# Products that nobody reads in TensorE's planned idle time, and new prices in the planner

## The chip, the cores and the metric

The kernel runs on one core of a Trainium2 chip. The metric is the device time of one execution in microseconds (us), the median of several runs. TensorE (PE in the views) multiplies matrices into the banks of PSUM, VectorE (DVE), ScalarE (ACT) and GpSimd (POOL) do the element-wise work, and SyncE (SP) issues the DMA transfers. Each engine works through its own instructions in the order in which the program lists them; semaphores hold an instruction back until what it needs is there.

## What is computed

One inference step of a decoder of four layers over a prompt of 512 tokens and eight samples of 8 tokens, at a width of 1024, all in fp32:

```python
def trunk(x, st_gla, st_gdn, st_conv, st_re, st_im, wts):
    for i in range(DEPTH):                      # DEPTH = 4
        kind = i % N_MIXERS                     # 0 GLA, 1 gated DeltaNet, 2 S5
        if kind == 0:
            f, s = gla_mixer(x, ...)
        elif kind == 1:
            f, cv, s = gdn_mixer(x, ...)
        else:
            f, hr, hi = s5_mixer(x, ...)
        x = layer_norm(ALPHA_RES * x + f, wts['ln_g'][i], wts['ln_b'][i])
```

Layers 0 and 3 are gated linear attention (GLA) with four heads, layer 1 is the gated DeltaNet with eight heads, a short convolution and a triangular solve in each chunk, layer 2 is an S5 state space with a gated linear unit (GLU) behind it. Each layer ends in an output product, a residual and a layer norm, and the next layer needs the result. The final states are outputs too.

## The kernel before

Every weight matrix is streamed in units of 128x1024 words (512 KB). A unit is split into a high and a low part (a cast and a subtraction, on ScalarE or VectorE), and each unit's *dense products* run as three f32r products with 288, 256 or 512 columns; one record of the trace is one such product. Their tile is `ps<-fx`. All other products (`ps<-sb`) are plain fp32 products, which leave two records each, or transposes, which leave one.

Layer 1 works in four pairs of heads. For a pair, the convolved k and q go through transposes and scores (`gdn_scores`: 128x128 transposes, then 128x256 products, eight for a pair), VectorE solves the diagonal blocks (`gdn_solve`), and the heads finish on TensorE (`gdn_head`: 128x96, 96x96, 64x64 and 128x128 products, each waiting for an evacuation of the one before). The convolution takes three taps on VectorE for each k, q or v unit. Layer 2 works in four pairs of S5 blocks: 128x72 products, a scan on VectorE, 128x72 products again, a trip through DRAM (`Ud`, `Yd`), and then the GLU, whose first three units wait for each eighth of that result. The tables for S5 are prepared earlier by `s5_prep0`, which fills time in layers 0 and 1; its last and largest part is `s5_prep`, four times.

The order on every engine is the work of a planner at build time. Python generators (threads, each with a rank) record operations; `record` finds what each depends on, `cost` gives it a price in us, and `run` keeps a clock of its own and issues on each engine the ready operation with the lowest rank. The thread `dense` has rank 10 and so fills what the rest leaves; the split of weights has rank 5, the chunk work of a layer 3 and up. The program that reaches the chip holds this order and the semaphores, but none of the planner's times. `cp` sends a copy to VectorE or ScalarE, whichever has less planned work. In the views nearly all instructions carry one line, L379 (L407 after the change), the call in `issue`.

Of the kernel before, what the change touches and what calls it, by code (L numbers as in the profile page):

```python
# [19 lines left out]
P = 128  # L20
# [122 lines left out]
FIXED = KT * 4 * HW + KT * P + RING * 2048 + 512 + 2 * HW + 512  # L143
WORDS = 52992 - FIXED
BLOCK = object()
ENGINES = ('PE', 'DVE', 'ACT', 'POOL', 'SP')
ACT_SETS = {
    AF.Exp: ('exp_and_others', 'natural_log_exp_and_others'), AF.Ln: ('natural_log_exp_and_others',),
# [20 lines left out]
class Engine:  # L169


    def __init__(self, core, name, real):
        self.core, self.name, self.real = core, name, real
# [10 lines left out]
class Core:  # L184
# [5 lines left out]
    def __init__(self, ctx, tc):  # L190
        nc = self.real = tc.nc
        self.fixed = ctx.enter_context(tc.tile_pool(name="fx", bufs=1)).tile([P, FIXED], F32R, name="fx")
        self.sb = ctx.enter_context(tc.tile_pool(name="sb", bufs=1)).tile([P, WORDS], F32, name="sb")
        self.ps = ctx.enter_context(tc.tile_pool(name="ps", bufs=1, space=PSUM)).tile([P, 4096], F32, name="ps")
        self.dram_pool = ctx.enter_context(tc.tile_pool(name="dram", bufs=1, space=DRAM))
        self.sb_name, self.ps_name = self.sb.tensor.name, self.ps.tensor.name
        self.vector, self.scalar = Engine(self, 'DVE', nc.vector), Engine(self, 'ACT', nc.scalar)
        self.gpsimd, self.tensor = Engine(self, 'POOL', nc.gpsimd), Engine(self, 'PE', nc.tensor)
        self.sync = Engine(self, 'SP', nc.sync)
        self.clock = dict.fromkeys(ENGINES, 0.0)  # L200
        self.dma = 0.0
        self.pending = dict.fromkeys(ENGINES, 0.0)
        self.queue = {e: ([], []) for e in ENGINES}
        self.ops, self.now, self.table = [], 0.0, None
        self.dense_backlog = 0

        self.region = {}
        for name, n, g in ((self.sb_name, WORDS, 16), (self.fixed.tensor.name, FIXED, 16), (self.ps_name, 4096, 32)):
            self.track(name, n, g, 4)
        self.spans, self.scratch = {}, {}  # L210
        self.bank_op = {e: np.full((4, 8), -1, np.int32) for e in ENGINES}
        self.constants = set()
        self.holes, self.used = [[0, WORDS]], {}
        self.banks = [False] * 8
        self.frees = 0
        self.threads, self.seq, self.events = [], 0, set()
        self.cur = [None, 0, 0, None, '', lambda: 0]


    def track(self, name, n, g, rows):  # L220
        new = lambda: np.full((rows, n // g), -1, np.int32)
        self.region[name] = (n, g, new(), {e: new() for e in ENGINES})

# [28 lines left out]
    def record(self, eng, method, fn, args, kw):  # L252
# [19 lines left out]
        for v in outs:  # L272
            s = self.span(v)
            if s is not None:
                _, _, w, r = self.region[v.tensor.name]
                order.update(np.unique(w[s]).tolist())
                for e in ENGINES:
                    order.update(np.unique(r[e][s]).tolist())
# [47 lines left out]
    def cost(self, op, method, args, kw, outs, ins):  # L326

        eng = op.eng
        column = any(v.shape[-1] == 1 for v in ins) or len(outs) > 1
        if not outs:  # L330
            op.cost, op.table = 1.28, args[0]
            return
        out = outs[0]
        size = lambda v: prod(v.shape[1:])
        n = size(out) if eng == 'PE' else max(size(v) for v in outs + ins)
        if eng == 'PE':
            m = 0.107 * size(ins[0]) / P if method != 'transpose' else 0.0
            if method == 'transpose':
                op.cost = n * 0.85e-3
            elif kw['lhsT'].dtype == F32R:  # L340
                op.cost = max(n * 0.417e-3, m)
            else:
                op.cost = 2 * max(n * 0.833e-3, m)
        elif eng == 'DVE':
            in_ps = any(v.tensor.name == self.ps_name for v in outs + ins)
            op.cost = 0.07 + n / 960.0 * (0.5 if not in_ps and method in ('tensor_copy', 'tensor_scalar') else 1)
            if column:
                op.cost += 0.06
        elif eng == 'ACT':
            sb = all(v.tensor.name != self.ps_name for v in ins)  # L350
            op.cost = 0.05 + 0.835e-3 * n + (0.043 if sb else 0.0) + (0.093 if column else 0.0)
            op.table = ACT_SETS.get(args[2] if len(args) > 2 else None)
        elif eng == 'POOL':
            op.cost = 0.3 + 0.165 * n if kw.get('op') == ALU.pow else 0.12 + 2.2e-3 * n
            if method == 'memset':
                op.cost = 0.1 + 0.6e-3 * n
        else:
            op.cost, op.tail = 0.45, prod(out.shape) * 4 / 360e3

    def issue(self, op):  # L360
        e = op.eng
        t = max(self.now, op.ready)
        if op.table is not None:
            sets = op.table if isinstance(op.table, tuple) else (op.table,)
            if self.table not in sets:
                self.table = sets[0]
                if isinstance(op.table, tuple):
                    t += 1.28
        self.clock[e] = t + op.cost
        op.end = t + op.cost  # L370
        if e == 'SP':
            self.dma = max(self.dma, op.end + 0.7) + op.tail
            op.end = self.dma + 1.0
        op.issued = True
        self.pending[e] -= op.cost
        if e == 'PE' and op.rank >= 10:
            self.dense_backlog -= 1
        fn, args, kw = op.call
        fn(*args, **kw)  # L379
        op.call = None  # L380
        for s, lat in op.succ:
            s.ready = max(s.ready, t if lat is None else op.end + lat)
            s.pend -= 1
            if not s.pend:
                heappush(self.queue[s.eng][0], (s.ready, s.seq, s))
        op.succ = None

    def writers(self, *aps):
        ids = set()
        for v in aps:  # L390
            s = self.span(v)
            if s is not None:
                ids.update(np.unique(self.region[v.tensor.name][2][s]).tolist())
        ids.discard(-1)
        return [self.ops[i] for i in ids]
# [31 lines left out]
    def A(self, *shape, dt=F32, long=False):  # L427
        keep = self.cur[5]
        while True:
# [3 lines left out]
            if v is not None:  # L433
                return v
            yield BLOCK

    def bank(self, n=1, held=None):

        while True:
# [9 lines left out]
            if best is None:  # L449
                yield BLOCK  # L450
                continue
# [68 lines left out]
    def run(self):  # L520
        while True:
            wake = []
            moved = True
            while moved:
                moved, wake = False, []
                for th in list(self.threads):
                    c = self.can_go(th)
                    if c is not True:
                        if c is not False:
                            wake.append(c)  # L530
                        continue
                    self.cur = th
                    moved = True
                    try:
                        v = next(th[0])
                    except StopIteration:
                        self.threads.remove(th)
                        continue
                    if v is BLOCK:
                        v = self.frees  # L540
                    elif isinstance(v, bass.AP):
                        v = self.writers(v)
                    elif isinstance(v, list):
                        v = self.writers(*v)
                    th[3] = v
                for e in ENGINES:
                    waiting, ready = self.queue[e]
                    while waiting and waiting[0][0] <= self.now + 1e-9:
                        _, s, op = heappop(waiting)
                        heappush(ready, (op.rank, s, op))  # L550
                    if ready and self.clock[e] <= self.now + 1e-9:
                        self.issue(heappop(ready)[2])
                        moved = True
            for e in ENGINES:
                waiting, ready = self.queue[e]
                if ready:
                    wake.append(self.clock[e])
                elif waiting:
                    wake.append(max(self.clock[e], waiting[0][0]))
            wake = [t for t in wake if t > self.now]  # L560
            if not wake:
                if not self.threads:
                    return
                raise AssertionError("nothing can go on: " + str([t[4] for t in self.threads]) + str(self.banks))
            self.now = min(wake)
# [1757 lines left out]
```

## Time and profile before

| | |
|---|---|
| time, median of 3 runs (lowest to highest) | 1359.83 us (1357.68 to 1359.98) |
| the profiled execution's own time | 1360.72 us |
| its span, first to last instruction | 1358.9 us |
| TensorE busy | 1274.3 us (94%) |
| VectorE busy | 953.4 us (70%) |
| ScalarE busy | 601.9 us (44%) |
| granted clock of TensorE, mean | 0.960 |

The span is that of one execution under the profiler; the time around it is 1.8 us. The granted clock is 1 at 2.4 GHz and 0.5 at 1.2 GHz. Busy time of TensorE is modelled, so an engine that is busy for the whole of a stretch may still hold short waits; the number of its records in a stretch says how fast it went.

### The profile page before, as it was taken

The page shows a single profiled execution, that of the slowest core. Times are in us where ns is not written, and L with a number is a line of the kernel's source. Part 1 is how long each engine was busy: PE and PEld are TensorE (multiplying, and loading weights), DVE is VectorE, ACT ScalarE, POOL GpSimd, SP SyncE. Part 2 cuts the span into 40 slices and gives each one's busy share as a digit, 9 for nine tenths or more (in the row PEclk, how much of TensorE's full clock was granted, in tenths as well). Part 3 has the DMA queues.
Part 4 walks back from the last instruction along what each step waited for, and adds up shares of the span by engine and source line. Part 5 has one row for each costly group of instructions (what it writes and reads, how often), then busy time and mean ns, then how long its engine had stood idle before and what let it go on. Part 6 is the DMA issues. An engine that isn't in the chain of part 4 may idle for free.

```text
span 1358.9 us, 23510 instructions
## 1 busy us (share of the span) xinstructions
PE 1274.3 (94%) x8795; PEld 1193.2 (88%) x8795; DVE 953.4 (70%) x2087; ACT 601.9 (44%) x1341; POOL 163.0 (12%) x303
## 2 busy tenths in 40 slices
PE   8999998989996798899999889999999999999997
PEld 8999997869895698799988788999998899999985
DVE  5888888798999788778678519355334867665557
ACT  5554355224855665534542224346123245443430
POOL 5510000021211121112101000000000200000001
PEclk8999999989996899899999888899999999999999
DMA  6335546334456826274374598773325332332342
GB/s 233 106 106 167 183 149 209 128 103 141 126 147 192 235 65 189 54 177 131 118 246 128 186 238 211 202 197 86 109 78 178 104 122 98 129 129 98 124 147 70
DMA packets 129538, 198.35 MB, mean 146 GB/s; under 512 B 47176, under 2 KB 85961, under 8 KB 127377
## 3 DMA queue, kind: packets, MB, share of 16 engines
q1 hardware_dynamic: 129424, 196.86, 48.0%
q8 instruction: 69, 1.13, 0.4%
q14 instruction: 45, 0.36, 0.1%
HBM read 153.64 MB, written 47.37 MB: 148 GB/s over the span
## 4 chain that ended last, share of the span: by engine, by line
PE 76%; DVE 12%; DMA 5%; ACT 3%; issue 2%; SPq 2%; POOLq 0%; POOL 0%; DVEq 0%; ACTq 0%
PE ps L379 76%; DVE sb L379 9%; DVE fx L379 3%; ACT sb L379 2%; SPq L379 2%; DMA sb<-scr 1%; DMA sb<-Ud 1%; DMA sb<-in_s_z 1%; ACT fx L379 1%; DMA out_conv<-sb 0%; DMA sb<-in_gla_s 0%; DMA Ud<-sb 0%; DMA sb<-in_xT 0%; DMA Yd<-sb 0%; DMA sb<-in_gdn_s 0%
## 5 line engine op out<-in xcount | busy, mean ns | idle before, releaser
L379 PE MATMUL ps<-fx 128*128 128x288 f32 (+2 forms) x6736 | 1048.6, 313 | 21.1 <-DVE fx L379 7.9
L379 PEld LDWEIGHTS ps<-fx 128*128 128x128 f32 x6736 | 957.0, 192 | 70.8 <-DVE fx L379 10.4
L379 ACT CAST fx<-sb 128x1024 fp32r<-128x1024 f32 (+5 forms) x318 | 227.2, 743 | 315.9 <-PE ps L379 277.0
L379 DVE TENSOR_TENSOR fx<-sb,fx 128x1024 fp32r<-128x1024 f32 (+5 forms) x308 | 253.2, 846 | 158.1 <-ACT fx L379 143.3
L379 PE MATMUL ps<-sb 128*128 128x128 f32 (+10 forms) x2059 | 302.5, 299 | 54.1 <-DVE sb L379 20.2
L379 PEld LDWEIGHTS ps<-sb 128*128 128x128 f32 (+6 forms) x2059 | 252.7, 180 | 85.2 <-ACT sb L379 24.2
L379 DVE TENSOR_TENSOR sb<-sb 128x128 f32<-128x128 f32 (+32 forms) x667 | 262.0, 416 | 20.6 <-ACT sb L379 6.5
L379 ACT COPY sb<-ps 128x512 f32<-128x512 f32 (+10 forms) x247 | 94.4, 404 | 158.8 <-PE ps L379 96.8
L379 DVE SCALAR_TENSOR_TENSOR sb<-sb 128x600 f32<-128x600 f32 (+7 forms) x205 | 133.8, 661 | 13.2 <-ACT sb L379 6.9
L379 ACT ACTIVATE sb<-sb 128x128 f32<-128x128 f32 (+10 forms) x241 | 108.0, 501 | 65.8 <-DVE sb L379 57.5
L379 DVE SCALAR_TENSOR_TENSOR sb<-sb,ps 128x256 f32<-128x256 f32 (+3 forms) x216 | 92.9, 458 | 61.3 <-PE ps L379 44.7
L379 POOL TENSOR_TENSOR sb<-sb 128x1 f32<-128x1 f32 (+4 forms) x46 | 75.8, 1653 | 468.4 <-DVE sb L379 446.1
L379 ACT ACTIVATE sb<-ps 128x128 f32<-128x128 f32 (+2 forms) x176 | 67.0, 385 | 73.7 <-PE ps L379 42.9
L379 DVE SCALAR_TENSOR_TENSOR sb<-ps,sb 128x128 f32<-128x128 f32 (+3 forms) x112 | 55.7, 505 | 44.3 <-PE ps L379 40.7
L379 DVE COPY sb<-ps 128x256 f32<-128x256 f32 (+6 forms) x85 | 34.2, 407 | 66.0 <-PE ps L379 36.7
L379 POOL COPY sb<-sb 128x24 f32<-128x24 f32 (+4 forms) x92 | 35.9, 413 | 280.0 <-DVE sb L379 161.5
L379 POOL MEMSET sb<- 128x8 f32 (+9 forms) x96 | 28.5, 315 | 203.7 <-DVE sb L379 143.7
L379 ACT ACTIVATE sb<-ps,sb 128x128 f32<-128x128 f32 (+2 forms) x98 | 40.7, 435 | 22.6 <-PE ps L379 21.8
L379 ACT CAST fx<-ps 128x512 fp32r<-128x512 f32 (+2 forms) x32 | 17.6, 550 | 72.5 <-PE ps L379 69.5
L379 ACT ACT_TABLE_LOAD x31 | 39.8, 1283 | 1.7 <-PEq L2312 0.7
L379 POOL CAST fx<-sb 128x32 fp32r<-128x32 f32 (+1 forms) x33 | 10.8, 357 | 217.8 <-PE ps L379 217.8
L379 ACT ACTIVATION_READ_ACCUMULATOR sb<-ps 128x1 f32 x136 | 27.8, 204 | 0.0
(25 smaller groups left out, 245.9 us busy)
## 6 DMA issues: line engine op xcount, KB each, us to landing
sb<-in_gla_v SPq DMA_DIRECT2D x16, 512.0 KB, 4.1
sb<-in_gla_r SPq DMA_DIRECT2D x16, 512.0 KB, 3.6
sb<-in_gla_s SPq DMA_DIRECT2D x8, 1024.0 KB, 5.7
out_s_gla<-sb SPq DMA_DIRECT2D x8, 1024.0 KB, 5.1
sb<-in_gla_out SPq DMA_DIRECT2D x16, 512.0 KB, 4.1
sb<-in_gdn_s SPq DMA_DIRECT2D x32, 256.0 KB, 3.2
sb<-in_s_glu SPq DMA_DIRECT2D x16, 512.0 KB, 3.7
xres<-sb SPq DMA_DIRECT2D x12, 512.0 KB, 4.5
```

Source lines behind the costliest of these rows:

```text
L379: fn(*args, **kw)
```

## The change

It has three parts. First, `cost` gives products other prices (a dense product with 288 columns 0.133 us instead of 0.120, a plain one slightly more) and prices a transfer by the length of its contiguous runs. Second, `granted` keeps account of planned idle time of TensorE, and `issue` doubles a product's price where the slice before held much of it. Third, `warm` is called when nothing on TensorE is ready: once a slice has used up a share of idle time, it records a plain fp32 product of 128x64 into a PSUM bank that nobody holds and whose last users have ended by the plan, again and again until something is ready. Nobody reads the result.

```diff
+WINDOW = 3.413
...
         if eng == 'PE':
-            m = 0.107 * size(ins[0]) / P if method != 'transpose' else 0.0
+            m = 0.111 * size(ins[0]) / P
             if method == 'transpose':
-                op.cost = n * 0.85e-3
+                op.cost = max(n * 0.867e-3, 0.06)
             elif kw['lhsT'].dtype == F32R:
-                op.cost = max(n * 0.417e-3, m)
+                op.cost = max(8e-3 + n * 0.434e-3, m)
             else:
-                op.cost = 2 * max(n * 0.833e-3, m)
+                op.cost = 2 * max(n * 0.843e-3, m, 0.055)
...
         else:
-            op.cost, op.tail = 0.45, prod(out.shape) * 4 / 360e3
+            run = min(self.run_of(v) for v in outs + ins)
+            op.cost, op.tail = 0.45, prod(out.shape) / run * (8e-3 + 0.188e-3 * run) / 16
...
+    def granted(self, t):
+
+        a = max(self.clock['PE'], t - 4 * WINDOW)
+        while a < t - 1e-6:
+            w = int(a / WINDOW + 1e-9)
+            e = min(t, (w + 1) * WINDOW)
+            self.idle[w] = self.idle.get(w, 0.0) + e - a
+            a = e
+        return self.idle.get(int(t / WINDOW) - 1, 0.0) < 0.4 * WINDOW
 
     def issue(self, op):
         e = op.eng
         t = max(self.now, op.ready)
+        if e == 'PE' and not self.granted(t):
+            op.cost *= 2
+            self.pending[e] += op.cost / 2
...
+    def warm(self):
+
+
+        if self.queue['PE'][1] or self.clock['PE'] > self.now + 1e-9 or not any(t[4] == 'dense' for t in self.threads):
+            return None
+        w = int(self.now / WINDOW + 1e-9)
+        left = 0.25 * WINDOW - self.idle.get(w, 0.0) - (self.now - max(self.clock['PE'], w * WINDOW))
+        if left > 1e-6:
+            return min(self.now + left, (w + 1) * WINDOW + 1e-6)
+        for b in range(8):
+            if not self.banks[b] and all(i < 0 or self.ops[i].issued and self.ops[i].end + 0.36 <= self.now
+                                         for e in ENGINES for i in self.bank_op[e][:, b].tolist()):
+                self.cur = [None, 0, 0, None, 'warm', lambda: 0]
+                self.tensor.matmul(self.ps[:, 512 * b:512 * b + 64], lhsT=self.ident, rhs=self.ident[:, 0:64],
+                                   start=True, stop=True)
+                return True
+        return self.now + 0.1
```

The program then has 8076 products on TensorE instead of 8010; the 66 new ones are `128x64`. Because every price feeds the planner, the order changes on all engines. VectorE gets 44 instructions more and ScalarE 49 fewer, table loads among them, since `cp` chooses anew.

On TensorE, in layer 1, this is what stood between the last scores of pair 0 (the first row) and those of pair 1. The 128x128 and 64x128 rows are pair 1's transposes and its samples' products, the 128x256 rows its scores, and 128x288 are dense products:

```order
L379 MATMUL ps<-sb 128x256 x4
L379 MATMUL ps<-fx 128x288 x179
L379 MATMUL ps<-sb 128x128 x10
L379 MATMUL ps<-sb 64x128 x2
L379 MATMUL ps<-sb 128x128 x4
L379 MATMUL ps<-fx 128x288 x12
L379 MATMUL ps<-sb 128x256 x2
L379 MATMUL ps<-fx 128x288 x14
L379 MATMUL ps<-sb 128x128 x4
L379 MATMUL ps<-fx 128x288 x20
L379 MATMUL ps<-sb 128x256 x2
L379 MATMUL ps<-fx 128x288 x2
```

And at the same place now:

```order
L407 MATMUL ps<-sb 128x256 x2
L407 MATMUL ps<-fx 128x288 x122
L407 MATMUL ps<-sb 128x128 x4
L407 MATMUL ps<-fx 128x288 x3
L407 MATMUL ps<-sb 128x128 x4
L407 MATMUL ps<-fx 128x288 x118
L407 MATMUL ps<-sb 128x128 x4
L407 MATMUL ps<-sb 128x256 x2
L407 MATMUL ps<-fx 128x288 x77
L407 MATMUL ps<-sb 128x128 x6
L407 MATMUL ps<-sb 64x128 x2
L407 MATMUL ps<-fx 128x288 x6
```

Pair 1's work came in one block behind 179 dense products; now its first head comes behind 122 and its second behind 243 to 320.

A little further on TensorE, pair 0's heads began like this (128x96 is a head's first product):

```order
L379 MATMUL ps<-fx 128x288 x67
L379 MATMUL ps<-sb 128x96 x4
L379 MATMUL ps<-fx 128x288 x9
L379 MATMUL ps<-sb 128x96 x4
L379 MATMUL ps<-sb 96x96 x4
L379 MATMUL ps<-sb 128x128
L379 MATMUL ps<-fx 128x288 x10
L379 MATMUL ps<-sb 96x96 x4
```

And now (the 128x64 rows are new products):

```order
L407 MATMUL ps<-fx 128x288 x145
L407 MATMUL ps<-sb 128x64 x8
L407 MATMUL ps<-sb 128x96 x8
L407 MATMUL ps<-sb 96x96 x8
L407 MATMUL ps<-sb 128x128
L407 MATMUL ps<-sb 128x64
L407 MATMUL ps<-sb 96x96 x8
L407 MATMUL ps<-sb 64x64 x4
```

From pair 0's last scores to its first 128x96 product there stood 294 dense products; now 511. Dense products no longer run between the head's steps, and new ones stand there.

On TensorE, in layer 2, the end of the S5 pairs (128x72), the u, z and GLU products (128x288) and the output product (128x512) stood like this:

```order
L379 MATMUL ps<-sb 128x72 x16
L379 MATMUL ps<-fx 128x288 x33
L379 MATMUL ps<-sb 128x72 x40
L379 MATMUL ps<-fx 128x288 x132
L379 MATMUL ps<-sb 128x72 x16
L379 MATMUL ps<-fx 128x288 x59
L379 MATMUL ps<-sb 128x72 x16
L379 MATMUL ps<-fx 128x288 x837
L379 MATMUL ps<-fx 128x512 x160
```

And now:

```order
L407 MATMUL ps<-sb 128x72 x40
L407 MATMUL ps<-fx 128x288 x74
L407 MATMUL ps<-sb 128x72 x8
L407 MATMUL ps<-fx 128x288 x151
L407 MATMUL ps<-sb 128x72 x16
L407 MATMUL ps<-fx 128x288 x47
L407 MATMUL ps<-sb 128x72 x16
L407 MATMUL ps<-fx 128x288 x52
L407 MATMUL ps<-sb 128x64 x3
L407 MATMUL ps<-fx 128x288 x660
L407 MATMUL ps<-sb 128x64 x5
L407 MATMUL ps<-fx 128x512 x153
```

The GLU has 768 dense products, and its last 660 need the last pair's result. Between them and the last 128x72 product there stood 177 dense products; now 52 and three new ones.

## Rows read from the trace of the kernel before

**Rows 1.** The page, part 1: busy time, share of the span, instructions.

```profile
span 1358.9 us, 23510 instructions
...
PE 1274.3 (94%) x8795; PEld 1193.2 (88%) x8795; DVE 953.4 (70%) x2087; ACT 601.9 (44%) x1341; POOL 163.0 (12%) x303
```

**Rows 2.** Windows by stage: stretch and length, busy time (records) by engine, granted clock, DMA.

```profile
34.00:272.00 238.00, 232.19 (x1675) 215.12 (x1675) 199.23 (x415) 112.48 (x246) 33.26 (x35) 0.99 0.46 150
282.00:340.00 58.00, 49.63 (x342) 45.55 (x342) 53.15 (x105) 25.70 (x44) 15.65 (x28) 0.94 0.38 125
340.00:400.00 60.00, 56.77 (x407) 55.34 (x406) 54.98 (x166) 44.53 (x107) 13.82 (x48) 0.97 0.52 142
400.00:447.00 47.00, 32.55 (x189) 29.82 (x188) 43.29 (x155) 26.27 (x75) 7.99 (x26) 0.78 0.66 191
447.00:580.00 133.00, 114.29 (x800) 106.03 (x799) 108.92 (x329) 77.53 (x246) 20.68 (x48) 0.90 0.47 127
803.00:868.00 65.00, 59.63 (x400) 58.91 (x401) 43.52 (x65) 25.19 (x60) 1.18 (x6) 0.82 0.88 231
```

**Rows 3.** Windows of the stretches at granted clock 0.5: four, and all 13 summed.

```profile
410.30:420.54 10.24, 5.23 (x19) 4.65 (x20) 10.00 (x49) 8.61 (x38) 0.46 (x5) 0.50 0.42 98
430.78:441.02 10.24, 7.82 (x28) 6.91 (x29) 10.09 (x43) 2.03 (x6) 2.92 (x7) 0.50 0.87 245
...
830.14:836.97 6.83, 5.26 (x22) 4.91 (x22) 5.78 (x9) 5.56 (x12) 0.00 (x0) 0.50 0.70 215
857.45:867.69 10.24, 10.24 (x48) 10.24 (x48) 2.94 (x5) 2.37 (x8) 0.33 (x2) 0.50 0.92 317
sum 102.41, PE 79.40 PEld 73.30 DVE 76.75 ACT 44.47 POOL 9.65; mean PE 6.11 PEld 5.64 DVE 5.90 ACT 3.42 POOL 0.74
```

**Rows 4.** Timeline, TensorE, 378 to 448 us: start, length, records, in brackets the wait.

```profile
378.67 1.89 PE L379 MATMUL ps<-sb 128*128 128x256 f32 x8
...
414.72 1.12 PE L379 MATMUL ps<-sb 128*128 128x128 f32 x4 [8.35 <-ACT sb L379]
416.43 1.81 PE L379 MATMUL ps<-fx 128*128 128x288 f32 x6 [0.59 <-DVE fx L379]
...
432.21 2.07 PE L379 MATMUL ps<-sb 128*128 128x256 f32 x4 [4.25 <-DVE sb L379]
435.28 1.09 PE L379 MATMUL ps<-fx 128*128 128x288 f32 x3 [0.99 <-DVE fx L379]
...
446.86 1.03 PE L379 MATMUL ps<-sb 128*128 128x96 f32 x8
```

**Rows 5.** Groups by form, VectorE: busy us, mean ns, idle before.

```profile
L379 DVE TENSOR_TENSOR fx<-sb,fx 128x1024 fp32r<-128x1024 f32 x143 | 174.2, 1220 | 120.8 <-ACT fx L379 107.2 <-DMA Yd<-sb 8.7 <-PE ps L379 3.8
...
L379 DVE SCALAR_TENSOR_TENSOR sb<-sb 128x600 f32<-128x600 f32 x72 | 60.0, 834 | 6.7 <-ACT sb L379 6.5
...
L379 DVE TENSOR_TENSOR sb<-sb 128x1024 f32<-128x1024 f32 x40 | 47.7, 1219 | 0.3
...
L379 DVE TENSOR_TENSOR sb<-sb 128x1152 f32<-128x1152 f32 x24 | 32.1, 1351 | 0.0
```

**Rows 6.** Windows, a stretch of layer 2 with 288-column dense products alone.

```profile
950.00:1020.00 70.00, 70.00 (x527) 70.00 (x526) 24.52 (x25) 15.42 (x17) 0.00 (x0) 1.00 0.30 93
```

**Rows 7.** Timeline, the last S5 products and the way of their result.

```profile
914.62 3.69 PE L379 MATMUL ps<-sb 128*128 128x72 f32 x32
...
919.02 3.85 SPq L379 DMA_DIRECT2D Yd<-sb  x8
...
924.83 0.37 SPq L379 DMA_DIRECT2D sb<-Yd  x1
```

**Rows 8.** DMA issues: count, KB each, median us from issue to landing.

```profile
sb<-Yd SPq DMA_DIRECT2D x4, 576.0 KB, 4.5
```

More of the change, by code (lines that the diff above doesn't have):

```diff
@@ L205, in __init__ @@
         self.dense_backlog = 0
+        self.idle = {}
         self.region = {}
@@ L357, in cost, with run_of @@
         else:
-            op.cost, op.tail = 0.45, prod(out.shape) * 4 / 360e3
+            run = min(self.run_of(v) for v in outs + ins)
+            op.cost, op.tail = 0.45, prod(out.shape) / run * (8e-3 + 0.188e-3 * run) / 16
+    def run_of(self, ap):
+        dims = list(ap.ap)
+        if ap.tensor.name in self.region:
+            dims = dims[1:]
+        n = 1
+        for step, num in reversed(dims):
+            if num > 1 and step != n:
+                break
+            n *= num
+        return n
+    def granted(self, t):
[6 more added lines that the diff above has]
+        return self.idle.get(int(t / WINDOW) - 1, 0.0) < 0.4 * WINDOW
     def issue(self, op):
@@ L553, in run @@
                         moved = True
+            t = self.warm()
+            if t is True:
+                continue
+            if t is not None:
+                wake.append(t)
             for e in ENGINES:
```

## The prediction

> **What bounds the kernel now.** I read the page first: TensorE is busy for 1274 of 1358.9 us [rows 1]. So most of the time is TensorE's own work, and only what it loses can be won. Where it loses, the windows by stage tell [rows 2]: from 34 to 272 us (layer 0) it is busy for 232.2 of 238 us, but from 400 to 447 us for 32.6 of 47, from 447 to 580 us for 114.3 of 133, and from 803 to 868 us for 59.6 of 65. The first two of these places are the chunks of the gated DeltaNet layer (layer 1), the third the S5 layer (layer 2). In the DeltaNet layer VectorE is the fuller engine: over 282 to 447 us it is busy for 53.2 + 55.0 + 43.3 = 151.4 of 165 us, which is 92%. The timeline shows what TensorE waits for there: 8.35 us for pair 1's products at 406 us, then 0.59, 4.25 and 0.99 us, 14.2 us in all [rows 4].
>
> The second loss is the clock. Besides the end, the granted clock is at its lower level (1.2 instead of 2.4 GHz) in 13 stretches of 102.4 us in all. TensorE is busy for 79.4 us of them; each stands behind such waits [rows 3]. Work done there takes at most half as long at the upper level, so a clock that never fell would be worth up to 39.7 us.
>
> The Trainium skill, on the page "TensorE: Matmul & The Clock Gate" (Part 1: The HAM clock gate), says of the cold start that "the ramp penalty is <1% of a typical kernel span". Taken as a bound on what the clock can give, that would be 13.6 us, an estimate from the page, and the rival below with the held clock could not happen. This trace disagrees: half of 79.4 us is 2.9% of the span, because here the clock falls again and again.
>
> **The change, part by part.** Two things happen: 66 products that nobody reads, and a whole new order on all engines, since the planner's prices changed.
>
> *The new products.* Each is a plain fp32 product, two records in the trace. Their nearest row is 32 records with 72 columns in 3.69 us [rows 7], 0.115 us each, so 0.23 us per product and 15.2 us for all 66. Along the new order 30 stand among the heads of pairs 0 and 1 and 10 in the layer norms between layers, where TensorE waits now; these cost nothing as long as the wait behind them is longer, and the largest group (8, 1.8 us) is shorter than the waits of rows 4. If that cover went they would cost 40 x 0.23 = 9.2 us. Some 20 stand where this trace shows TensorE without a wait (the first weights, layer 0, the output product of layer 1, the end of the GLU): 20 x 0.23 = **+4.6 us**. Bounds 0 and 15.2.
>
> *The corrected price of a dense product.* The planner took 0.120 us for a 288-column product and now takes 0.133. The trace has 527 in 70 us, 0.133 us [rows 6], so TensorE's price is now right. VectorE's price stays, and is too low: a 128x1024 subtraction is planned at 1.14 us and takes 1.22, a 600-column tap at 0.76 and takes 0.83 [rows 5]. The plan thus still believes VectorE's chains shorter than they are.
>
> *Layer 1 up to the heads of pair 0.* Between pair 0's last scores and its first head product the old order has 294 dense products (39 us), the new one 511 (68 us). In the trace this stretch took from 380 to 447 us, 67 us [rows 4], so the new order has filler for all of it. The second head of pair 1, for which TensorE waited 8.35 us, now comes after 243 to 320 dense products instead of 179. But the heads start when VectorE is through. It loses the last quarter of S5's preparation, which moves into layer 0: 6 of the 24 128x1152 products and 5 of the 128x1024 ones, 6 x 1.35 + 5 x 1.22 = 14.2 us [rows 5]. It gains the work of dense units that now come earlier: when pair 0's heads start, 169 more dense products stand ahead, 3.5 units of 48, each with a split (1.22) and three taps (0.83), 3.7 us, so 13.1 us. The stretch keeps its length but for 1.1 us, at 92% **-1.2 us**. Bounds: -14.2, if all four waits go, and +2.6.
>
> *Heads of pairs 0 and 1 (447 to 580 us).* The filler was pulled ahead, so 159 dense products stand here instead of 378: 29.1 us less for TensorE, and 6.9 us of new products. It is left with 114.3 - 29.1 + 6.9 = 92 us, VectorE with 108.9 - 13.1 = 95.8 us. If the round trips between the engines set the pace, the stretch stays 133 us. If VectorE were as full as in the stretch ahead (92%), it would take 104 us. I take this stretch's own share (108.9 of 133, 82%), the nearest row: 117 us, a gain of 16. At its end TensorE stands 50 dense products further back than in the old order, 6.6 us that are paid later, where it is the bound. Together **-9.4 us**, bounds -22 and +6.6.
>
> *Layer 0.* The 14.2 us of S5's preparation, with some scaled copies, come on top of VectorE's 199.2 us from 34 to 272 us: 90% full, nearly the share at which TensorE lost most in layer 1. Bounds 0 and 14.2 us; most of it fits into the 38.8 us that VectorE has free, so I take **+4 us**.
>
> *Layer 2.* The products of the S5 pairs stand 20 to 125 dense products later among the u and z products, so the 5.4 us of waits from 803 to 868 us may go, and with them half of the 5.26 and 10.24 us of work at the lower clock [rows 2, 3]: 13.1 us. In exchange only 52 dense products (6.9 us) stand between the last S5 product and the GLU products that need its result. In the trace the eight stores of it are issued until 922.9 us and the load back at 924.8, 6.5 us after the product's end [rows 7]; the load lands 4.5 us later [rows 8], and a cast and a subtraction of 512 columns follow, which I estimate at 0.7 us each from the 1.22 us of 1024 columns [rows 5]. That is 12.4 us, so a new wait of 5.5 us, and one more fall of the clock, 3.4 us by half of a stretch like 830 to 837 us. The old order had 177 products of cover there (69 that are not GLU's and 108 of GLU's own) and no wait. **-4.2 us**, bounds -13 and +8.9.
>
> Elsewhere (layer 3, the other falls of the clock) I take nothing; half of what stands in the other low stretches is at most 25 us. The sum is 4.6 - 1.2 - 9.4 + 4 - 4.2 = -6.2 us. The profiled execution took 1360.7 us, 0.9 above the median of 1359.8, so 1354.5 for a profile and **1354 us** for the median, 0.4% less.
>
> **The rivals.** *The clock is held.* If the new products bridge what is left of the waits, all 39.7 us come back; with all 15.2 us of new products on the path that is 1360.7 - 24.5 = 1336 us. Against it: the clock fell behind waits of 8.35 and 4.25 us, and 8 products fill 1.8.
>
> *The chain without filler (slower).* In the heads of pairs 0 and 1 the products wait for VectorE and ScalarE at each step, and the dense products that ran in between are gone. If the stretch keeps its 133 us, its term is +6.6 instead of -9.4: 4.6 - 1.2 + 6.6 + 4 - 4.2 = +9.8, so 1370 us. It decides when that stretch shrinks by less than 9.8 us. For it speaks that VectorE's prices stay too low while TensorE's went up, so TensorE reaches each product that waits sooner than VectorE delivers.
>
> *It does not do what it says.* The waits move, the clock falls about as often, and order and added products cancel: 1360 us. For it: 66 products of 0.23 us are little beside 102 us of low clock.
>
> **How the numbers follow.** The forecast has 0.42, the held clock 0.13, the cancelled change 0.15, the chain without filler 0.30. Under 0.2% (2.7 us) a measurement of this kernel tells nothing from no change; so 0.55 faster, 0.15 same, 0.30 slower. The forecast's own range is 1346 to 1357. The bounds of the terms move the outer cases by some 6 us each: 1330 to 1376 us for 8 in 10.
>
> **What would show it.** Right: TensorE's idle time from the scores to the heads of pair 0 is gone, pair 1's heads end some 10 to 15 us earlier, a new wait of 5 to 6 us stands before the last first-GLU products, and low-clock stretches are fewer in the S5 layer. Wrong: pair 0's heads start later than now by more than 10 us, the heads take 133 us or more, or TensorE's idle time in layer 0 grows past 15 us.

## The result and the profile after

The changed kernel takes 1371.88 us (median of 4 runs, 1367.84 to 1373.87) where the kernel before took 1359.9 beside it: a ratio of 1.0094, 95% interval 1.0067 to 1.0121. It is slower by 0.9%; the forecast was 0.4% faster. The page of its profiled execution, part 1:

```profile
span 1368.9 us, 23838 instructions
...
PE 1289.2 (94%) x8927; PEld 1206.1 (88%) x8927; DVE 968.3 (71%) x2131; ACT 583.5 (43%) x1292; POOL 164.5 (12%) x303
```

TensorE has 132 records more than in [rows 1], two for each of the 66 products, and is busy for 14.9 us more; the span grew by 10.1. The windows of the changed kernel by stage (columns as in [rows 2]): layer 0, the first norm, layer 1 as a whole, then its part between pair 0's scores and heads, the part of the heads of pairs 0 and 1 and the part behind them, the second norm, and the end of S5 with the start of the GLU:

```profile
34.00:272.00 238.00, 226.68 (x1676) 207.87 (x1674) 209.28 (x423) 112.24 (x246) 30.93 (x35) 1.00 0.48 154
287.20:344.30 57.10, 52.92 (x339) 48.45 (x339) 55.34 (x146) 23.05 (x38) 17.86 (x31) 0.97 0.36 124
344.30:759.50 415.20, 380.54 (x2632) 353.42 (x2632) 333.05 (x924) 212.57 (x591) 71.90 (x160) 0.95 0.51 144
386.60:468.50 81.90, 76.68 (x569) 75.63 (x567) 74.32 (x182) 50.84 (x119) 22.78 (x55) 0.99 0.66 172
468.00:569.00 101.00, 86.27 (x601) 78.64 (x602) 80.57 (x274) 58.16 (x201) 13.46 (x27) 0.89 0.41 106
569.00:759.00 190.00, 182.81 (x1244) 166.60 (x1243) 139.50 (x352) 76.18 (x200) 26.71 (x49) 0.98 0.48 142
759.50:804.20 44.70, 41.46 (x313) 40.98 (x312) 21.30 (x31) 13.96 (x17) 1.17 (x2) 1.00 0.92 263
936.00:971.00 35.00, 29.43 (x205) 29.00 (x205) 11.14 (x14) 10.19 (x13) 0.00 (x0) 0.90 0.35 96
```

The same for the kernel before: layer 1 as a whole, its part between pair 0's scores and heads, its part behind the heads of pairs 0 and 1, and the second norm:

```profile
340.60:745.40 404.80, 367.43 (x2524) 341.19 (x2524) 331.40 (x952) 219.61 (x622) 67.27 (x165) 0.94 0.53 150
...
380.00:447.00 67.00, 52.55 (x337) 49.76 (x336) 61.33 (x213) 38.18 (x99) 13.45 (x48) 0.85 0.64 172
...
579.00:745.00 166.00, 165.02 (x1147) 151.14 (x1146) 125.07 (x305) 71.47 (x197) 25.50 (x44) 1.00 0.54 159
...
745.40:803.10 57.70, 45.62 (x313) 43.44 (x311) 24.52 (x36) 15.69 (x20) 1.71 (x3) 0.91 0.74 207
```

The second norm has 313 records in both kernels; they took 57.7 us before and take 44.7 now, and the clock does not fall. That gain was not forecast. Layer 1 takes 10.4 us more. The stretch from pair 0's scores to its heads grew from 67 to 81.9 us, the heads of pairs 0 and 1, which took 133, take 101, and the part behind them takes 190 where it took 166.

For all kernels below I worked out from the trace what TensorE *lost* in a stage: the length of the stage less its records, each at the median spacing that its form has at the upper clock in the trace before. Waits and lower clock are both in it; the new products count as work, not as loss. "At lower clock" is the time at granted clock 0.5, here with the end of the program, which the prediction's 102.4 us left out. In us, with the stages cut at the same places of the program:

| | products | at lower clock | layer 0 | two norms | layer 1 | S5 | GLU start | rest |
|---|---|---|---|---|---|---|---|---|
| before | 0 | 111.0 | 18.9 | 27.8 | 69.7 | 16.1 | 0.1 | 22.4 |
| after | 14.6 | 88.8 | 26.5 | 11.1 | 66.4 | 18.2 | 8.2 | 20.2 |

All losses fell from 155.1 to 150.7, by 4.4 us; the 66 products brought 14.6 us of records: together the 10.1 us of the spans.

Two new waits, on the timeline of TensorE in the changed kernel (columns as in [rows 4]):

```profile
363.82 3.36 PE L407 MATMUL ps<-fx 128*128 128x288 f32 x24
374.46 4.95 PE L407 MATMUL ps<-sb 128*128 128x128 f32 x18 [7.29 <-DVE sb L407]
...
461.13 1.67 PE L407 MATMUL ps<-sb 128*128 128x64 f32 x14
465.28 0.43 PE L407 MATMUL ps<-sb 128*128 128x64 f32 x2 [2.48 <-DMA sb<-scr]
468.46 5.97 PE L407 MATMUL ps<-sb 128*128 128x96 f32 x35 [2.75 <-DMA sb<-gcd]
...
936.18 7.16 PE L407 MATMUL ps<-fx 128*128 128x288 f32 x52
943.18 0.78 PE L407 MATMUL ps<-sb 128*128 128x64 f32 x6
948.90 0.58 PE L407 MATMUL ps<-fx 128*128 128x288 f32 x1 [4.94 <-DVE fx L407]
```

At 374 us the products of pair 0's scores wait 7.29 us for VectorE, and 13.7 us at the lower clock go with it; before, the longest wait at that place was 3.0 us. At 943 us three new products run after the 52 dense ones and then the GLU waits 4.94 us. What it waits for, on SP's queue (issues of transfers):

```profile
937.10 5.01 SPq L407 DMA_DIRECT2D Yd<-sb  x8
...
944.32 0.38 SPq L407 DMA_DIRECT2D sb<-Yd  x1
```

and, once the load has landed, on VectorE:

```profile
948.13 0.62 DVE L407 CAST fx<-sb 128x512 fp32r<-128x512 f32 x1 [19.73 <-DMA sb<-Yd]
```

From the end of the last S5 product (936.4) to the first product that has its result (948.9) it is 12.5 us; the prediction had 12.4.

### The profile page after: what moved, and what is told of

Its sections match the earlier page's. It is cut to its first block, busy times and chain, and to the rows that moved or that the text cites. A ratio compares the mean times of both kernels' runs of the same rounds, so it can differ in the third digit from the quotient of the medians.

```text
span 1368.9 us, 23838 instructions
## 1 busy us (share of the span) xinstructions
PE 1289.2 (94%) x8927; PEld 1206.1 (88%) x8927; DVE 968.3 (71%) x2131; ACT 583.5 (43%) x1292; POOL 164.5 (12%) x303
## 5 line engine op out<-in xcount | busy, mean ns | idle before, releaser
L407 PE MATMUL ps<-fx 128*128 128x288 f32 (+2 forms) x6736 | 1053.6, 313 | 18.9 <-DVE fx L407 7.3
L407 PE MATMUL ps<-sb 128*128 128x128 f32 (+9 forms) x2191 | 321.9, 297 | 52.6 <-DVE sb L407 27.2
L407 ACT CAST fx<-sb 128x1024 fp32r<-128x1024 f32 (+5 forms) x311 | 223.1, 743 | 330.2 <-PE ps L407 278.8
L407 PEld LDWEIGHTS ps<-sb 128*128 128x128 f32 (+5 forms) x2191 | 270.9, 181 | 83.7 <-DVE sb L407 33.5
L407 DVE TENSOR_TENSOR sb<-sb 128x128 f32<-128x128 f32 (+28 forms) x667 | 266.1, 416 | 19.3 <-ACT sb L407 6.4
L407 ACT COPY sb<-ps 64x256 f32<-64x256 f32 (+11 forms) x242 | 94.4, 409 | 148.8 <-DVE sb L407 72.9
L407 ACT ACTIVATE sb<-sb 128x128 f32<-128x128 f32 (+8 forms) x234 | 105.8, 503 | 67.4 <-DVE sb L407 59.5
L407 POOL COPY sb<-sb 128x24 f32<-128x24 f32 (+4 forms) x92 | 43.1, 491 | 317.7 <-DVE sb L407 113.5
L407 ACT ACTIVATE sb<-ps,sb 128x128 f32<-128x128 f32 (+2 forms) x76 | 33.2, 449 | 23.9 <-PE ps L407 21.2
L407 DVE TENSOR_SCALAR sb<-ps,sb 128x128 f32<-128x128 f32 (+2 forms) x58 | 23.6, 417 | 8.0 <-ACT sb L407 6.4
```

## The experiments

The theories that the expectations name. **P**: the products are TensorE's time on the path. **C**: they hold the clock up and pay for themselves. **O**: the new order costs 8 us in layer 0 and 8 at the GLU. **S**: any change of a price makes another order, and orders scatter by 10 us or more, so no part of the change has a price of its own. **G**: the doubled price spoils the order. **I**: doubled price and products together do. **N**: what the right price of a product gives in every order lies in the norms.

All runs, timed in five rounds beside the kernel before (1356.1 to 1360.1 us in these groups). "Cover" is the number of dense products between the last S5 product and the GLU products that need its result; the losses are those of the profiled execution, one for each run. The executions of one and the same order scatter too, by 5 to 17 us: e3's twelve go from 1342.1 us at a mean granted clock of 0.982 to 1359.2 at 0.967, and its losses are those of the slowest; e17's are those of the fastest of its twelve (1340.3).

| run | products | cover | median us | ratio, 95% interval | lower clock | layer 0 | norms | layer 1 | GLU start |
|---|---|---|---|---|---|---|---|---|---|
| e1 changed, products not issued | 0 | 52 | 1364.45 | 1.0059, 1.0034 to 1.0084 | 78.0 | 29.3 | 13.3 | 68.9 | 8.2 |
| e2 new prices alone | 0 | 91 | 1339.50 | 0.9877, 0.9850 to 0.9904 | 70.9 | 31.3 | 6.3 | 53.5 | 6.5 |
| e3 changed, old transfer price | 45 | 221 | 1348.44 | 0.9940, 0.9914 to 0.9966 | 93.0 | 34.9 | 11.0 | 49.6 | 0.2 |
| e4 before, with products and doubling | 78 | 225 | 1359.95 | 1.0030, 1.0007 to 1.0052 | 75.0 | 29.6 | 19.3 | 54.4 | 0.2 |
| e5 changed, no doubling | 66 | 108 | 1339.94 | 0.9870, 0.9842 to 0.9898 | 68.0 | 27.3 | 8.0 | 44.0 | 3.1 |
| e6 changed, no products | 0 | 132 | 1346.84 | 0.9914, 0.9885 to 0.9943 | 72.4 | 26.5 | 8.1 | 69.6 | 0.1 |
| e7 as e2, price 0.1326 | 0 | 178 | 1339.22 | 0.9867, 0.9836 to 0.9897 | 59.1 | 24.1 | 6.1 | 59.1 | 1.9 |
| e8 as e2, price 0.1334 | 0 | 42 | 1352.54 | 0.9968, 0.9943 to 0.9994 | 97.0 | 29.0 | 4.7 | 62.1 | 11.2 |
| e9 changed, price 0.1326 | 108 | 76 | 1382.97 | 1.0189, 1.0152 to 1.0227 | 95.1 | 24.9 | 6.5 | 77.8 | 1.9 |
| e10 changed, price 0.1334 | 63 | 180 | 1338.96 | 0.9867, 0.9830 to 0.9904 | 62.4 | 27.3 | 10.1 | 47.0 | 0.1 |
| e11 before, price 0.1197 | 0 | 88 | 1351.40 | 0.9952, 0.9926 to 0.9977 | 96.4 | 15.9 | 23.1 | 71.1 | 5.6 |
| e12 before, price 0.1205 | 0 | 103 | 1349.50 | 0.9934, 0.9906 to 0.9961 | 96.8 | 24.7 | 22.8 | 53.5 | 1.6 |
| e13 e9, products not issued | 0 | 76 | 1379.59 | 1.0135, 1.0084 to 1.0186 | 118.9 | 24.7 | 5.1 | 99.1 | 3.2 |
| e14 e10, products not issued | 0 | 180 | 1341.29 | 0.9850, 0.9809 to 0.9890 | 75.1 | 28.1 | 10.8 | 59.7 | 0.1 |
| e15 before, new product prices | 0 | 219 | 1345.12 | 0.9881, 0.9838 to 0.9924 | 78.9 | 27.4 | 5.7 | 64.2 | 0.2 |
| e16 e5, price 0.1334 | 73 | 166 | 1332.83 | 0.9796, 0.9753 to 0.9838 | 53.1 | 25.5 | 13.7 | 36.0 | 1.4 |
| e17 e5, price 0.1326 | 74 | 131 | 1345.87 | 0.9927, 0.9899 to 0.9955 | 57.3 | 23.6 | 6.6 | 53.1 | 0.1 |
| e18 changed, price 0.1321 | 70 | 23 | 1351.99 | 0.9983, 0.9964 to 1.0001 | 56.7 | 26.6 | 4.0 | 51.3 | 11.6 |

**The products alone: e1, e13, e14.** The planner records, prices and orders the new products as ever; at the end they are left out of the program, and the rest keeps its order. Nobody reads them, so nothing else is missing.

```diff
+        op.dead = self.cur[4] == 'warm'
...
-        fn(*args, **kw)
+        if not op.dead:
+            fn(*args, **kw)
```

> The changed kernel in its very order, but the 66 new products are planned and then not issued. Theory P (the products are TensorE's own time on the path nearly everywhere): the 14.5 us of their records go, 1357 us. Theory C (they keep the clock up, so they pay for themselves): the stretches at the lower clock grow from 88.8 us towards the 111 us of before, and the time stays at 1370 to 1375. My own reading, by the gaps behind each group in the trace of the changed kernel: 25 of the 66 stand where TensorE had no wait behind them, 6 to 8 us, so 1364 to 1366.

> The slowest order so far (the whole change with the product at 0.1326 us, 1383 us), in which the 108 new products are planned and not issued. Theory P (the 44 us between the two orders of the whole change are mostly the products, 108 against 63): 23.8 us of records go, 1359 us. Theory S (they are the order's): the share that the first such run showed, 43% of the records' time, goes, 10 us, so 1373 us.

> The fastest order of the whole change (the product at 0.1334 us, 1339 us), its 63 new products planned and not issued. Theory C (here the products hold the clock up and are the gain): the stretches at the lower clock grow from 62 us by 15 or more, 1342 to 1350. Theory S: 43% of 13.9 us of records go, 1333 us.

In the changed kernel the products cost 6.2 us of span (1368.9 to 1362.7) of 14.6 us of records; the ratios, 1.0094 and 1.0059, give 4.8, plus or minus 5.0 by their intervals. In the slowest order, with 23.8 us of records, the spans show no cost (1378.3 with them, 1379.3 without), but the ratios give 7.3, plus or minus 8.6; in the fastest of the whole change, with 13.9 us of records, they give 2.3, plus or minus 7.5. So P fell: in none of the three orders do the records come off the time in full, by the intervals at most some two thirds of them do. Whether the share is nothing or as much as the 43% that S had for e13 and e14 is not resolved; S's times for them, 1373 and 1333 us, were 7 and 8 us too low. Layer 1 of e9, with its products, in windows:

```profile
337.20:793.60 456.40, 415.39 (x2881) 387.94 (x2881) 355.14 (x980) 226.84 (x618) 70.19 (x165) 0.94 0.49 145
```

and of e13, without them:

```profile
335.80:791.50 455.70, 396.23 (x2680) 366.67 (x2680) 355.27 (x980) 226.84 (x618) 72.35 (x165) 0.91 0.49 145
```

201 records go, TensorE is busy for 19 us less, VectorE's 980 instructions take the same 355 us, and the stage keeps its 456 us. The products filled waits there, and the clock that goes with them (0.94 against 0.91) comes with no shorter stage. As far as one execution of each shows, what sets the length of this stage is not TensorE's own work. One place shows it, the first head product, in e9 and then in e13:

```profile
452.98 11.50 PE L407 MATMUL ps<-sb 128*128 128x96 f32 x69 [4.54 <-DMA sb<-scr]
```

```profile
450.12 3.91 PE L409 MATMUL ps<-sb 128*128 128x96 f32 x17 [9.42 <-DMA sb<-scr]
```

It waits for a load in both, 115.8 and 114.3 us after the stage's start; the 15 new products that stand ahead of it in e9 only shorten the wait. C is half right: without the products the lower clock does grow, by 24 us in e13 and 13 in e14 (the mean granted clock of all executions goes from 0.963 to 0.960 and from 0.978 to 0.974), but no change of the time is clear of its interval; in e1 it shrank.

**Parts of the change: e2 to e6, e15.** e2 has neither products nor doubling, e5 no doubling, e6 no products, e3 the old price of a transfer; e4 has the old prices of products and transfers, with new products and doubling, e15 the new prices of TensorE's products and nothing else of the change.

```diff
-            t = self.warm()                     # e2, e6, e15
+            t = None
...
-        if e == 'PE' and not self.granted(t):   # e2, e5, e15
-            op.cost *= 2
-            self.pending[e] += op.cost / 2
+        if e == 'PE':
+            self.granted(t)
...
-            op.cost, op.tail = 0.45, prod(out.shape) / run * (8e-3 + 0.188e-3 * run) / 16   # e3, e4, e15
+            op.cost, op.tail = 0.45, prod(out.shape) * 4 / 360e3
...
-                op.cost = max(8e-3 + n * 0.434e-3, m)   # e4, with the two other prices of products
+                op.cost = max(n * 0.417e-3, m)
```

> New prices of products and transfers, no new products and no doubled prices. It has 91 dense products between the last S5 product and the GLU products that need it (52 in the changed kernel, 177 before), and S5's preparation ends at dense product 1382 (1357 and 1563). Theory O (the new order costs 8 us in layer 0 and 8 us at the GLU): without the products but with both of these places, 1358 to 1362, and a wait of about 1 us before the GLU, since 39 more products cover 5.2 of the 5.6 us. Theory P: all the loss was the products, 1357 or less.

> The changed kernel with the old price of a transfer; 45 new products are left, and 221 dense products stand between the last S5 product and the GLU. Theory O: the wait of 5.6 us before the GLU and the 6.8 us at the lower clock behind it go, 8 us, and 21 products fewer give 3 to 5 more: 1359 to 1361. Theory S (any change of prices makes a new order whose time scatters by 10 us, and no single price is the cause): anywhere from 1355 to 1375, whatever the GLU does.

> The kernel before with the new products and the doubled prices, but the old prices of products and transfers; 78 new products, 225 dense products of cover before the GLU. Theory P: 78 x 0.22 = 17 us more than before, less what lies in waits, so 1367 to 1377. Theory O: the products lie in waits and the order has not got the new prices, so 1357 to 1364.

> The changed kernel without the doubled price behind planned idle time: new prices and 66 new products. Against the new prices alone (1339.5 us) theory P (the products, which the planner issues as work of TensorE, take the path or push other work back) gives 6 to 15 us more, 1346 to 1354. Theory G (the doubled price is what spoils the order) gives the products' own 6 to 8 us that the run with the products left out showed, 1345 to 1348. Theory S (any new order scatters by 10 us): anywhere from 1335 to 1365.

> The changed kernel without the new products, the doubled price kept, planned anew. Theory G: the doubled price spoils the order, so it stays where the changed kernel with its products left out stood, 1360 to 1366. Theory P: without products the new prices gain what they gained alone, 1337 to 1343. By its order (132 dense products of cover before the GLU, pair 0's heads at dense product 2288) I expect it nearer to the second, 1340 to 1348.

> The kernel before with the new prices of TensorE's products alone; 219 dense products of cover before the GLU. Theory N (what the right price of a product gives in every order is the wait in the two layer norms, 6 to 11 us lost there with new prices and 23 to 28 with old ones, against 6 to 8 us more in layer 0): norms at 5 to 11 us lost, layer 0 at 24 to 31, no wait at the GLU; the whole by the scatter of layer 1, 1335 to 1352. If the gain came from the price of a transfer: 1352 to 1362 and norms as before.

The new prices alone are 1.2% faster than the kernel before. Products on top leave that as it is (e5), the doubling alone takes perhaps some of it (e6, 0.4%, but the intervals overlap), and both together lose all of it and more (the changed kernel). Taken at its word that is theory I. O missed e2: it had 1358 to 1362 us and some 1 us of wait at the GLU, where 1339.5 came and 6.5 us were lost. It hit e4 (1357 to 1364), where P had 1367 to 1377. e3 speaks for O at the GLU, whose wait goes as expected (0.2 us lost); but the median came out 11 us below the 1359 to 1361 that O had (some 8 by the ratio), and the S5 stage of its profiled execution, its slowest, lost 27.1 us where the changed kernel's lost 18.2: stages move that nobody meant to touch.

e15 bears out N. All four kernels with the old price of a product lose 19 to 28 us in the two norms, all sixteen with the new one (thirteen orders) 4 to 14, e15 among them. Its windows of the two norms:

```profile
288.90:338.90 50.00, 48.66 (x327) 44.88 (x326) 46.85 (x114) 23.02 (x38) 11.59 (x33) 1.00 0.38 126
723.90:782.20 58.30, 55.62 (x371) 51.72 (x370) 35.73 (x59) 18.86 (x24) 7.05 (x13) 1.00 0.73 218
```

The clock stays at 1.00 where the kernel before had 0.94 and 0.91. Since e15 moves the prices of dense and plain products and of transposes at once, it does not show which of them matters. In exchange layer 0 loses 24 to 35 us with the new price (before and in e11 19 and 16, but in e12 25 and in e4 30).

**Is one order a measurement of the change? e7 to e12, e16 to e18.** The planner's price of a 288-column product is moved by a third of a per cent, e18's by twice that. The chip does the same work, in another order.

```diff
-                op.cost = max(8e-3 + n * 0.434e-3, m)
+                op.cost = max(8e-3 + n * 0.4355e-3, m)   # e8, e10, e16; 0.4325 in e7, e9, e17; 0.431 in e18
...
-                op.cost = max(n * 0.417e-3, m)
+                op.cost = max(n * 0.4155e-3, m)          # e11; 0.4185 in e12
```

> New prices alone, with the 288-column product at 0.1326 us in place of 0.1330 (a third of a per cent less): a change that means nothing for the chip, but makes another order (178 dense products of cover before the GLU, pair 0's heads at 2217). Theory S: the time moves by 5 us or more from 1339.5, either way. If a right price makes the gain: 1336 to 1343, and no wait before the GLU takes 3 to 5 us off.

> New prices alone, with the 288-column product at 0.1334 us. Its order has 42 dense products of cover before the GLU, fewer than the changed kernel's 52, so a wait of 6 to 7 us and 6.8 us of lower clock stand there. If a right price makes the gain: 1339.5 and 3 to 5 us for the longer wait, 1342 to 1346. Theory S: 5 us or more away from that.

> The whole change with the 288-column product at 0.1326 us in place of 0.1330. Its planner adds 108 products instead of 66; 76 dense products of cover before the GLU. Theory I (doubled price and products together spoil the order, whatever the rest): 1365 to 1378, as the changed kernel, and 5 us more for 42 more products. Theory S (the 1371.9 us are one draw out of orders that scatter by some 10 us around the 1339 to 1352 us of the runs with new prices): 1340 to 1360, of which the GLU's wait takes about 5.

> The whole change with the 288-column product at 0.1334 us; 63 new products and 180 dense products of cover before the GLU, so no wait there (8 us less than the changed kernel at that place). Theory I: 1360 to 1368. Theory S: 1338 to 1356.

> The kernel before with its 288-column product at 0.1197 us in place of 0.1201; 88 dense products of cover before the GLU (177). If the old prices themselves cost the 17 us that the new ones gained: 1356 to 1368, of which 5 to 7 for the GLU's wait. Theory S (the kernel before is one draw as well): anywhere from 1340 to 1372.

> The kernel before with its 288-column product at 0.1205 us; 103 dense products of cover before the GLU, so a wait of 2 to 4 us there. If the old prices cost 17 us: 1356 to 1366. Theory S: anywhere from 1340 to 1372, and more than 5 us away from the kernel with the product at 0.1197.

> New prices and 73 new products without the doubled price, the 288-column product at 0.1334 us; 166 dense products of cover before the GLU. Theory G (without the doubled price the order is good whatever the rest): 1335 to 1345. Theory S: anywhere from 1335 to 1380.

> New prices and 74 new products without the doubled price, the 288-column product at 0.1326 us; 131 dense products of cover before the GLU. Two orders without the doubled price took 1340 and 1333 us. Theory G (the doubled price is what makes the bad orders): 1330 to 1345. Theory S: with a chance of a half outside of that, up to 1380.

> The whole change with the 288-column product at 0.1321 us; 70 new products, 23 dense products of cover before the GLU, the fewest of all, so a wait of 8 to 10 us there and a fall of the clock. Three orders of the whole change took 1339, 1372 and 1383 us. Theory G: 1360 to 1385. Theory S: 1340 to 1385, the GLU's wait adding some 10 in any case.

S holds for the spread, which is wider than I had it: e9 came out 23 us above S's range, e3 and e16 7 and 2 us below theirs. It missed where it promised a move: e7 stayed at 1339.2 beside e2's 1339.5, and e11 and e12 are 1.9 us apart, where it had 5 us or more. The whole change, with prices at most 1% apart that say nearly the same of the chip, takes 1338.96, 1351.99, 1371.88 or 1382.97 us: 44 us apart, and on both sides of the kernel before. With it I falls (e10 has both parts and gains 1.3%). The new prices alone span 13 us (e2, e7, e8), the old ones 10 (the kernel before, e11, e12). Layer 1 of e10, in windows, to be held against that of e9 above:

```profile
343.60:739.80 396.20, 375.17 (x2636) 348.98 (x2636) 332.09 (x942) 219.81 (x615) 64.83 (x160) 0.97 0.54 154
```

Same heads, same chains, 60 us less in that stage; 245 records fewer, some of them new products, some work that stands outside of the stage in this order, are 29 us of it, and the loss is 30.8 us smaller.

G stays open. Four orders of the whole change average 1361 us, three of it without the doubling 1340 (1332.83 to 1345.87), but the two sets overlap, and G missed the range that it gave in each of the five runs that name one: e5, e6, e16 and e18 came out 2 to 13 us below it, e17 1 us above. The clock that the doubling reckons with is often not the one granted: of the changed kernel's products 128 were priced double in the plan and 72 of these ran at the lower clock, where the trace has 204 in all.

e18 shows the other sure cost, the cover. TensorE's timeline at the GLU of e18, with 23 dense products of cover:

```profile
925.71 0.58 PE L407 MATMUL ps<-fx 128*128 128x288 f32 x1 [6.73 <-DVE fx L407]
926.92 7.09 PE L407 MATMUL ps<-fx 128*128 128x288 f32 x35 [0.63 <-DVE fx L407]
```

Losses at the start of the GLU are 11.6, 11.2, 8.2 and 6.5 us with 23, 42, 52 and 91 dense products of cover, and 0.1 to 3.1 with 103 and more; 76 and 88 gave 1.9 to 3.2 and 5.6. So some 100 products (13 us) cover the trip of 12.5 us.

## Why the prediction was wrong

The sign was wrong: -6.2 us were forecast, +10.1 came in the spans. Term by term:

- **The new products**, +4.6 (bounds 0 and 15.2): 6.2 by e1's span, 4.8 plus or minus 5.0 by the ratios. The price of a record held (0.112 us spacing at the upper clock; I had 0.115). That the number is near is luck as far as the two traces go: layer 1, where 41 of the 66 stand and where I had those among the heads cost nothing, is 6.6 us shorter in e1, while no other stage is more than 2 us shorter.
- **Layer 0**, +4 (0 to 14.2): the loss grew by 7.6 us, and seven new products (1.6 us) stand there. VectorE is busy for 209.3 us there where it was for 199.2, and TensorE's waits for VectorE grew from 4.4 to 7.2 us: mechanism as forecast, size nearly double.
- **Up to the heads of pair 0**, -1.2: the stretch grew from 67 to 81.9 us, and the heads start 21.6 us later, the very sign that the prediction named as wrong. Its rule, "the heads start when VectorE is through", held: VectorE is busy for 74.3 of the 81.9 us, 91% as before (92% was taken), and for 86 to 96% of this stretch in the traces of all twenty kernels, in which it lasts 63.5 to 86.9 us and TensorE is busy for 63 to 97% of it. TensorE is nearly as full here (76.7 us), but VectorE waits for it for 1.2 us in all. The failed step is VectorE's work in it: the sum had 1.1 us less, and it grew by 13.0. Twelve more taps and six more splits came, 17.4 us (13.1 forecast), but the 14.2 us of S5's preparation that were to go had never stood there: before, the last of its 128x1152 products ran from 304 to 311 us. The filler did remove the waits (loss 21.6 to 5.9 us), though a wait of 7.29 us came ahead of the stretch, where I took nothing.
- **Heads of pairs 0 and 1**, -9.4: the stretch shrank to 101 us, further than the 117 forecast, and pair 1's heads end 10.0 us earlier (10 to 15 forecast). Here too the share held (VectorE 80% busy; 82% taken) and the work did not: 80.6 us, where I had 95.8. The two stretches together went from 200 to 182.9 us, 17.1 less, with 17.2 forecast before the debt; that is luck, since the less came from S5's preparation in the sum, and that was in neither stretch. VectorE's work went behind pair 1's heads instead, where it grew from 125.1 to 139.5 us. This is the second failed step: the sum held a debt of 6.6 us there, 50 dense products, and the part took 24 us more. TensorE, which had been busy for all but 1 of its 166 us, had 67 dense products more in it and lost 9.8 us more. So layer 1 took 10.4 us more in all, where the sum had it 10.6 shorter.
- **Layer 2**, -4.2: the new wait at the GLU came as worked out (8.1 us lost against 8.9 forecast, 12.5 us of trip against 12.4). What failed is the gain of 13.1 us in the S5 pairs, "waits from 803 to 868 us may go": S5 lost 18.2 instead of 16.1 us. The clock falls three times there as before (at 804, 832 and 866 us; at 803, 830 and 857), and was to fall less often. TensorE's waits in the changed kernel are for the transfer through DRAM, three of them, the first (2.9 us) just ahead of the first S5 product, as the view of waits by engine says (us in total, times, longest):

```profile
PE ps L407 <- DMA sb<-Ud: 8.5, 3, 3.6
```

- **Elsewhere "I take nothing"**: the norms lost 16.7 us less, as large a miss as any, to the good side.
- **VectorE's price.** "VectorE's price stays, and is too low" was a misreading. Two rows of VectorE in the trace before:

```profile
747.44 1.22 DVE L379 TENSOR_TENSOR fx<-sb,fx 128x1024 fp32r<-128x1024 f32 x1
748.57 0.74 DVE L379 SCALAR_TENSOR_TENSOR sb<-sb 128x512 f32<-128x512 f32 x1
```

The subtraction lasts 1.22 us, but the next instruction starts 1.13 us after it: the last 0.09 us overlap. The planner's 1.14 is the spacing, and right. So the new prices made TensorE's right beside a right VectorE, where the old ones had TensorE 10% too fast, and what I gave as a reason for the slower rival was none. (Of the clock the prediction says that work takes "at most half as long" at the upper level; at least half is meant, which makes 39.7 us an upper bound.)

The slower rival's time, 1370 us, was close, but by another way: it was to decide when the stretch from 447 to 580 us shrinks by less than 9.8 us, and that shrank by 32.

By the lengths of the stages, each with its new products, it was +4.5 us up to the first norm, -13.8 in the norms, +10.4 in layer 1 and +9.0 from the first S5 product to the end.

Beyond the terms: a sum over one order could not carry this. The same change made by prices at most 1% apart ends between 1.3% faster and 1.9% slower, and each of its orders has its own waits in layer 1 (47 to 78 us lost). What the runs show of the cause is therefore this: of the 10.1 us, 14.6 are records of products, of which some 5 cost time (0 to 10 by the intervals); the GLU costs 8 by too little cover; the norms give 17 back, as they do in every order with the new prices of products, and layer 0 takes 8; layer 1 and S5, which hold most of what is lost, come out as this one order has them. Which of the planner's choices makes an order good in layer 1 stays open, and so does whether the doubled price makes bad ones likelier.

The fastest order found is e16, the change without the doubled price: 2.0% below the kernel before (interval 1.6 to 2.5%). It too is one draw; e5 and e17 of the same kind gained 1.3 and 0.7%.

## What to carry to other kernels

Where a planner sets the order, measure a change of its costs over several orders (move a price by a fraction of a per cent) before it is credited or blamed: here one order of the whole change would have given any verdict from -1.3 to +1.9%. Products that only fill waits cost little and give little where other engines set the length of a stage (e9 and e13). Where one engine's work sets when the next chain starts, count that work in each stretch of the old trace before taking any of it away: here VectorE's 14.2 us were taken from a stretch in which they had never stood. Count the filler at each place where a result makes a trip (100 dense products for 12.5 us here).

## What the runs showed of the hardware that I had not expected

VectorE's instructions overlap: the 128x1024 subtraction lasts 1.22 us and the next one starts after 1.13. A higher granted clock need not come with a shorter stage: layer 1 of e9 and e13 takes 456.4 and 455.7 us at a mean of 0.94 and 0.91, in e9 with 201 records more. And the clock that one and the same program is granted differs between executions, and the time with it: 0.982 and 1342.1 us, 0.967 and 1359.2 us in e3.
